# Branch phase in written order, and attention merges moved from the triangular inverse to the scan

## The chip, the cores and the metric

The kernel runs on one core of a Trainium2 chip. A core has TensorE (matrix products into the accumulators of PSUM), VectorE (DVE), ScalarE (ACT), GpSimd (POOL), and SyncE (SP), which here issues nearly all transfers between the device's main memory and the core's own memory SBUF. Each engine, and SP's queue of transfers, works through its instructions strictly in order: an instruction that waits holds up all that stand behind it on the same engine. The metric is the device time of one execution in microseconds (us); less is better.

## The reference, cut to what matters

One decoder layer over 2048 tokens of width 1024. Branch A is a gated delta rule with a 64-token chunk, which needs the inverse of a triangular 64 x 64 matrix per chunk and head, and then a scan over 16 pairs of chunks. Branch B is windowed attention in three groups with different dilation; the groups are merged by their softmax denominators. Both are gated, projected, merged by sigmoid gates, and projected out:

```
o_dn  = gated_delta_rule_chunked(dq, dk, dv, g, beta)        # inverse, then scan
y_dn  = (rms_norm(o_dn, dn_norm_w) * silu(dn_z)) @ w_branch_dn
outs, lses = three groups of dilated_window_attention(...)
alpha = softmax(stack(lses), axis=0)                          # the merge of groups
o_swa = sum(alpha[..., None] * stack(outs), axis=0)
y_swa = (o_swa * silu(swa_z)) @ w_branch_swa
merged = sigmoid(g_dn) * y_dn + sigmoid(g_swa) * y_swa        # the branch phase
x     = x + merged @ w_out                                    # the output groups
```

All of it is in float32. A product of two float32 matrices is made of three passes over operands split in a high and a low part (names ending in h and l).

## The kernel before

The program is written as a sequence of matmul loops with a clock of **ticks**. `hook()` advances the tick and runs whatever was booked with `at(delay, fn)` for that tick, so work for the other engines is written between the matmuls. `flush()` turns the clock without matmuls until nothing is booked. A planner then orders the instructions of each engine and of the transfer queue: it plays the program with its own costs and lets an instruction go when its inputs are ready, earlier-written ones first. Inside a `manual_schedule` block the named engines keep the written order instead; `pinned(False)` names TensorE, ACT, DVE and POOL, and `pinned(True)` SP's transfers as well.

The last stages, in order:

- **Units** (`cunits`, the matmuls of L723 to L725): 36 column blocks of the input projection, four pieces of 512 tokens each, 16 ticks a block. Beside the later ones run the inverse and the scan. A gate unit ends in `g_block` (L1158, a tanh on ACT) and a store to `gscr`; a weight block is split by ACT and POOL (L90, L91).
- **Inverse** (`inverse`, L1023 to L1026): 63 rows of ever longer DVE work. Row i books row i+1 after about its expected duration in ticks. The inverse starts 9 ticks into unit 15 (counted from 0). ACT and POOL keep the written order in it (the block `ipin`).
- **Merges** (`comb_setup`, `comb_load`, `comb_min`, `combine`): 16 merges, one for each 128 tokens. A merge loads 780 KB of group outputs (L1243, two buffers), takes the minimum on DVE (L1248), computes weights on POOL and ACT (L1259 to L1267), scales twelve tiles on ACT (L1271), adds them in two POOL operations (L1275) and stores the result to `osd`. Merge 0 starts 11 ticks after the setup, the others 15 ticks apart. The setup is called where the inverse starts.
- **Scan** (`scan`, L1061 to L1123): 16 steps of three ticks, the first 29 ticks after its start. A step's chain goes from TensorE to DVE (`rr`, L1087), TensorE (L1094), ACT (`vn`, L1096), TensorE (L1100) and DVE (`S`, L1102); a norm on ACT and POOL (L1112 to L1119) ends in a DVE scaling (L1121) and a store (L1123). `zs` (L1064) prepares the next step.
- **Branch phase** (`fin_y`): 8 blocks of 256 tokens, in each 8 tiles of 128 channels. A tile is two ticks: 12 matmuls for each branch (L1341 to L1343). Its gates come in a tile `gt` of 256 KB from `gscr` (`g_load`, L1329, seven buffers, issued four tiles ahead). DVE gates the product (L1345), POOL adds the branches (L1347), and SP stores 128 KB to `mscr` (L1348) out of the same `gt` buffer. For the next block `o_plan` loads `z` (L1303, three buffers) and `o` (L1293), transposes on TensorE at ticks 4, 7, 10 and 13 of the block (L1310), multiplies on DVE (L1311) and splits on ACT and POOL (L1314, L1315) into the operands of the block. In the first blocks `wo_chunk` prepares four chunks of the output weight, 28 ticks apart; the parts T1 and T4 go through the single buffers `th` and `tl` to main memory.
- **Output groups** (`group`, L1420): 8 groups of 84 matmuls.

The branch phase and the output groups are ordered by the planner alone. The pools of `th`, `tl` and of the second weight buffers open after those of the merges close.

Of the kernel before, what the change touches and what calls it, by code (L numbers as in the profile page):

```python
# [12 lines left out]
P = 128  # L13
# [34 lines left out]
class Net:  # L48
# [951 lines left out]
    def inverse(self, ip, done):  # L1000
# [12 lines left out]
        def row(i):  # L1013
            if i == 64:
                nc.sync.dma_start(dr(self.vscr, 0, [[4096, P], [1, 4096]]), M.rearrange("p c i -> p (c i)"))
                zt = Z.rearrange("p (i c) -> p i c", c=64)
                for r in (slice(0, 32), slice(32, 64)):
                    V.tensor_copy(zt[:, r, :], M.rearrange("p c i -> p i c")[:, r, :])
                nc.sync.dma_start(dr(self.tscr, 0, [[4096, P], [1, 4096]]), Z)
                done()  # L1020
                return
            pr = Z[:, :i * i].rearrange("p (c j) -> p c j", j=i)
            V.tensor_tensor(out=pr, in0=M[:, 0:i, 0:i], in1=M[:, i, 0:i].unsqueeze(1).to_broadcast([P, i, i]), op=ALU.mult)  # L1023
            V.memset(M[:, i, :], 0.0)
            V.memset(M[:, i, i:i + 1], 1.0)
            V.tensor_reduce(out=M[:, 0:i, i:i + 1], in_=pr, axis=mybir.AxisListType.X, op=ALU.add)  # L1026
            self.at(max(1, round((2 * i * i / 960.0 + 0.5) / 1.3)), lambda: row(i + 1))
# [205 lines left out]
    def comb_setup(self, cb):  # L1233
        self.cb = cb
        self.mone = cb.tile([P, 4], F32, name="mone", bufs=1)
        self.nc.gpsimd.memset(self.mone, -1.0)
        self.comb_load(0)
        self.at(6, self.comb_min)
        self.at(11, lambda: self.combine(0))

    def comb_load(self, t):
        oc = self.oc = self.cb.tile([P, G, H, 130], F32, name="oc", bufs=2)
        self.nc.sync.dma_start(oc.rearrange("p g h c -> p (g h c)"),  # L1243
                               dr(self.oscr, t * P * G * H * 130, [[G * H * 130, P], [1, G * H * 130]]))

    def comb_min(self):
        self.cs = self.cb.tile([P, 4, 12], F32, name="cs", bufs=2)
        self.nc.vector.tensor_reduce(out=self.cs[:, 0, 0:4].unsqueeze(2), in_=self.oc[:, :, :, 128].rearrange("p g h -> p h g"),  # L1248
                                     axis=mybir.AxisListType.X, op=ALU.min)

    def combine(self, t):
        nc, cb, V = self.nc, self.cb, self.nc.gpsimd
        oc, sm = self.oc, self.cs
        if t < 15:
# [28 lines left out]
        if t < 15:  # L1283
            self.at(9, self.comb_min)
# [46 lines left out]
    def fin_y(self, nb, m):  # L1331
        nc = self.nc
        self.g_load(8 * nb + m + 4)
# [14 lines left out]
        nc.sync.dma_start(dr(self.mscr, nb * P * 2048 + m * 256, [[2048, P], [1, 256]]), gt[:, 0, :])  # L1348
# [95 lines left out]
    def run(self):  # L1444
# [60 lines left out]
        pin, ipin = ExitStack(), ExitStack()  # L1505
# [10 lines left out]
        def start_inverse():  # L1516
            self.nb_out()
            pin.close()
            ipin.enter_context(tc.manual_schedule(engines={E.Activation, E.Pool}))
            dst.close()  # L1520
            self.comb_setup(pool(bst, "cb"))
            self.inverse(pool(ist, "ip", "right"), start_scan)

        def start_scan():
            ipin.close()
# [38 lines left out]
        for j in range(4):  # L1564
            self.g_load(j)
        for nb in range(8):
            if nb < 7:
                self.o_plan(nb + 1, 4)
            if nb == 0:
                for c in range(4):  # L1570
                    self.at(1 + 28 * c, lambda c=c: self.wo_chunk(c))
            if nb == 7:
                self.m_load(0)
            for m in range(8):
                self.fin_y(nb, m)
                if nb == 7 and m in (1, 3):
                    self.fetch("T1" if m == 1 else "T4")
                if nb == 7 and m < 4:
                    self.at(4, lambda m=m: self.m_op(m))
        self.flush()  # L1580
# [49 lines left out]
```

## Time and profile before

| | |
|---|---|
| time, median of 3 runs | 2402.06 us (2399.08 to 2407.04) |
| the profiled execution's own time | 2403.63 us |
| its span, from first to last instruction | 2401.8 us |
| granted TensorE clock, mean | 0.983 of full speed |
| TensorE busy | 2289.9 us, 95% of the span |
| DVE, ACT, POOL busy | 57%, 41%, 44% |
| transfers | 485.82 MB, mean 202 GB/s |
| first inverse work to last (DVE, L1023 to L1026) | to 1669.6 us |
| scan's matmuls (L1083) | 1702.5 to 1868.7 us |
| branch phase's matmuls | 1990.3 to 2238.1 us |

A row of a profile names the source line (L1341), the engine, and the tiles as output<-input. PE is TensorE, SPq the transfer queue of SP. A wait's row names who waited, on whom, us in total, times, and the longest. The granted clock is the share of full speed at which TensorE was allowed to run.

### The profile page before, as it was taken

Reading aid. Unit: us, or ns where it says so; the run is one execution under the profiler, and the core shown is the slowest. Engines: PE = TensorE matmul, PEld = TensorE weight load, DVE = VectorE, ACT = ScalarE, POOL = GpSimd, SP = SyncE. Lnnn points to the kernel's source line nnn. Section 1 sums busy time; section 2 is a strip of 40 time slices with the busy share of each in tenths; the row PEclk is TensorE's granted clock in tenths of the full one; section 3 lists DMA queues with packets and bytes.
Section 4 is the critical chain, followed back from the end, with each engine's and each line's share of the span. In section 5 each row is a group of like instructions: output and inputs, shape, how many; then the busy total and the mean of one; then the engine's idle time right before and its main releaser. Section 6 shows DMA issues by size and latency. Waiting matters only on the chain. (4 is left out here: it accounts for less than half of the span.)

```text
span 2401.8 us, 43873 instructions
## 1 busy us (share of the span) xinstructions
PE 2289.9 (95%) x15120; PEld 2078.5 (87%) x15120; DVE 1358.6 (57%) x2786; ACT 978.8 (41%) x3151; POOL 1050.3 (44%) x1460
## 2 busy tenths in 40 slices
PE   7999999989999999999999999998999998897999
PEld 7999999989999999787788788886888888896787
DVE  6566586693545545537777759997244114522553
ACT  5345466642434435445666633333443222200221
POOL 5374275574303213305567544666333214532543
PEclk8999999999999999999999999999999999998999
DMA  9989988858887888744545434444777637765742
GB/s 290 328 280 307 282 276 273 260 166 271 257 255 238 260 260 282 217 141 120 131 114 132 112 110 132 133 127 138 228 212 195 200 113 203 215 171 161 255 155 92
DMA packets 557270, 485.82 MB, mean 202 GB/s; under 512 B 68280, under 2 KB 517112, under 8 KB 554104
## 3 DMA queue, kind: packets, MB, share of 16 engines
q1 hardware_dynamic: 556760, 482.95, 66.0%
q8 instruction: 120, 1.97, 0.3%
q14 instruction: 102, 0.84, 0.1%
q10 hardware_dynamic: 288, 0.07, 0.0%
HBM read 280.23 MB, written 202.67 MB: 201 GB/s over the span
## 5 line engine op out<-in xcount | busy, mean ns | idle before, releaser
L723 PE MATMUL mm<-hh,w 128*128 128x512 f32 x1152 | 463.5, 402 | 7.6 <-ACT gt L1158 7.6
L725 PE MATMUL mm<-hh,w 128*128 128x512 f32 x1152 | 458.0, 398 | 1.6 <-POOL w L91 1.6
L724 PE MATMUL mm<-hl,w 128*128 128x512 f32 x1152 | 457.2, 397 | 0.0
L436 PE MATMUL mm<-w,hh 128*128 128x256 f32 x1760 | 327.9, 286 | 0.0
L436 PEld LDWEIGHTS mm<-w,hh 128*128 128x128 f32 x1760 | 270.9, 189 | 0.0
L723 PEld LDWEIGHTS mm<-hh,w 128*128 128x128 f32 x1152 | 220.4, 191 | 54.0 <-ACT gt L1158 8.0
L725 PEld LDWEIGHTS mm<-hh,w 128*128 128x128 f32 x1152 | 217.1, 188 | 49.1 <-POOL w L91 2.1
L436 PE MATMUL mm<-hh 128*128 128x256 f32 x880 | 256.4, 291 | 0.0
L724 PEld LDWEIGHTS mm<-hl,w 128*128 128x128 f32 x1152 | 217.5, 189 | 42.4
L436 PE MATMUL mm<-hl,hh 128*128 128x256 f32 x880 | 248.8, 283 | 0.4 <-POOL hl L298 0.3
L436 PE MATMUL mm<-hh,hl 128*128 128x256 f32 x880 | 248.6, 283 | 0.0
L436 PE MATMUL mm<-w,hl 128*128 128x256 f32 x880 | 248.1, 282 | 0.0
L91 POOL TENSOR_TENSOR w<-raw,w 128x512 fp32r<-128x512 f32 x68 | 103.3, 1522 | 224.0 <-ACT w L90 216.3
L610 DVE CUSTOM_DVE_ANT_0 p<-sc,mask 128x128 f32<-128x128 f32 (+1 forms) x192 | 70.1, 365 | 213.0 <-PE sc L607 83.4
L371 POOL TENSOR_SCALAR st<-st 128x4 f32<-128x4 f32 x96 | 20.9, 218 | 373.1 <-ACT junk L370 371.1
L436 PEld LDWEIGHTS mm<-hl,hh 128*128 128x128 f32 x880 | 168.2, 191 | 0.8 <-POOL hl L298 0.8
L436 PEld LDWEIGHTS mm<-hh 128*128 128x128 f32 x880 | 168.2, 191 | 0.0
L436 PEld LDWEIGHTS mm<-hh,hl 128*128 128x128 f32 x880 | 168.0, 191 | 0.0
L436 PEld LDWEIGHTS mm<-w,hl 128*128 128x128 f32 x880 | 165.9, 189 | 0.0
L594 ACT ACTIVATE kq<-tp 128x256 fp32r<-128x256 f32 x148 | 56.5, 381 | 183.1 <-PE tp L587 182.3
L837 DVE SCALAR_TENSOR_TENSOR acc<-xr,cw,acc 128x512 f32<-128x512 f32 x144 | 120.9, 840 | 17.3 <-ACT acc L835 11.8
L613 ACT ACTIVATE p<-p,ol 128x128 f32<-128x128 f32 (+1 forms) x192 | 88.1, 459 | 62.5 <-DVE ol L610 62.2
(352 smaller groups left out, 5888.9 us busy)
## 6 DMA issues: line engine op xcount, KB each, us to landing
wdr<-w SPq DMA_DIRECT2D x56, 512.0 KB, 4.9
w<-wdr SPq DMA_DIRECT2D x54, 512.0 KB, 5.3
qk<-qks SPq DMA_DIRECT2D x212, 128.0 KB, 4.0
qks<-rec SPq DMA_DIRECT2D x96, 256.0 KB, 3.0
raw<-in_w_in_dram SPq DMA_DIRECT2D x68, 256.0 KB, 3.7
gscr<-gt SPq DMA_DIRECT2D x64, 256.0 KB, 3.2
gt<-gscr SPq DMA_DIRECT2D x64, 256.0 KB, 4.1
wdr<-hh SPq DMA_DIRECT2D x28, 512.0 KB, 4.4
```

Source lines behind the costliest of these rows:

```text
L91: eng.tensor_tensor(out=l, in0=raw, in1=h.bitcast(F32), op=ALU.subtract)
L371: nc.gpsimd.tensor_scalar(out=st[:, 0:4], in0=st[:, 0:4], scalar1=1.0 / P, scalar2=EPS, op0=ALU.mult, op1=ALU.add)
L436: mm = lambda x, y, **kw: nc.tensor.matmul(o, x, y, skip_group_check=True, **kw)
L594: nc.scalar.activation(h, src, AF.Copy)
L610: nc.vector.tensor_tensor_reduce(out=p[:, lo:hi], in0=sc[:, lo:hi], in1=self.mask[:, slot * P + lo:slot * P + hi], scalar=3e38, scale=-SCA ...
L613: self.at(1, lambda: nc.scalar.activation(p[:, lo:hi], p[:, lo:hi], AF.Exp, bias=ol[:, 128:129], scale=-1.0, accum_out=ol[:, 129:130]))
L723: nc.tensor.matmul(pr, wh[:, k, :], a, start=(k == 0), stop=False)
L724: nc.tensor.matmul(pr, wh[:, k, :], b, start=False, stop=False)
L725: nc.tensor.matmul(pr, wl[:, k, :], a, start=False, stop=(k == KT - 1))
L837: nc.vector.scalar_tensor_tensor(out=acc, in0=xr[:, j:j + 512], scalar=w[:, j:j + 1], in1=acc, op0=ALU.mult, op1=ALU.add)
```

## The change

Two things are altered.

1. The branch phase's eight blocks and the flush after them run inside `pinned(True)`: all four engines and SP's transfers keep the written order. The store of a tile (L1348) is booked two ticks after the tile instead of being issued at once, and the gates are loaded three tiles ahead instead of four (three loads before the loop instead of four).
2. `comb_setup` is called at the end of the inverse (row 64), after its two stores are written and before the scan is; both first loads are issued there. A copy of one column of the inverse's result into each of the first two buffers makes their loads wait for the inverse. From merge 1 on, merge t issues the load of merge t+1 as before. The block `ipin`, in which ACT and POOL kept the written order during the inverse, is gone.

```
@@ inverse, row 64
                 nc.sync.dma_start(dr(self.tscr, 0, [[4096, P], [1, 4096]]), Z)
+                self.comb_setup(M)
                 done()
@@
-    def comb_setup(self, cb):
-        self.cb = cb
-        self.mone = cb.tile([P, 4], F32, name="mone", bufs=1)
+    def comb_setup(self, M):
+        self.M, self.ocs = M, {}
+        self.mone = self.cb.tile([P, 4], F32, name="mone", bufs=1)
         self.nc.gpsimd.memset(self.mone, -1.0)
         self.comb_load(0)
-        self.at(6, self.comb_min)
+        self.comb_load(1)
+        self.at(6, lambda: self.comb_min(0))
         self.at(11, lambda: self.combine(0))

     def comb_load(self, t):
-        oc = self.oc = self.cb.tile([P, G, H, 130], F32, name="oc", bufs=2)
+        oc = self.ocs[t] = self.cb.tile([P, G, H, 130], F32, name="oc", bufs=2)
+        if t < 2:
+            self.nc.vector.tensor_copy(oc[:, 0, 0, 0:1], self.M[:, 63, 63:64])
         self.nc.sync.dma_start(oc.rearrange("p g h c -> p (g h c)"),
...
     def combine(self, t):
         nc, cb, V = self.nc, self.cb, self.nc.gpsimd
-        oc, sm = self.oc, self.cs
-        if t < 15:
+        oc, sm = self.ocs.pop(t), self.cs
+        if 0 < t < 15:
             self.comb_load(t + 1)
...
         if t < 15:
-            self.at(9, self.comb_min)
+            self.at(9, lambda: self.comb_min(t + 1))
             self.at(15, lambda: self.combine(t + 1))
@@
     def fin_y(self, nb, m):
         nc = self.nc
-        self.g_load(8 * nb + m + 4)
+        self.g_load(8 * nb + m + 3)
...
-        nc.sync.dma_start(dr(self.mscr, nb * P * 2048 + m * 256, [[2048, P], [1, 256]]), gt[:, 0, :])
+        self.at(2, lambda: nc.sync.dma_start(dr(self.mscr, nb * P * 2048 + m * 256, [[2048, P], [1, 256]]), gt[:, 0, :]))
@@ run
-        pin, ipin = ExitStack(), ExitStack()
+        pin = ExitStack()
...
             pin.close()
-            ipin.enter_context(tc.manual_schedule(engines={E.Activation, E.Pool}))
             dst.close()
-            self.comb_setup(pool(bst, "cb"))
+            self.cb = pool(bst, "cb")
             self.inverse(pool(ist, "ip", "right"), start_scan)

         def start_scan():
-            ipin.close()
             ist.close()
...
-        for j in range(4):
+        for j in range(3):
             self.g_load(j)
-        for nb in range(8):
+        with pinned(True):
+            for nb in range(8):
...
-        self.flush()
+            self.flush()
         fst.close()
```

More of the change, by code (lines that the diff above doesn't have):

```diff
@@ L1231, in fetch, with comb_min @@
             self.nc.sync.dma_start(a.bitcast(F32).rearrange("p k c -> p (k c)"), dr(self.wpk[n, x], 0, [[2048, P], [1, 2048]]))
-    def comb_setup(self, cb):
-        self.cb = cb
-        self.mone = cb.tile([P, 4], F32, name="mone", bufs=1)
+    def comb_setup(self, M):
+        self.M, self.ocs = M, {}
+        self.mone = self.cb.tile([P, 4], F32, name="mone", bufs=1)
         self.nc.gpsimd.memset(self.mone, -1.0)
         self.comb_load(0)
-        self.at(6, self.comb_min)
+        self.comb_load(1)
+        self.at(6, lambda: self.comb_min(0))
         self.at(11, lambda: self.combine(0))
     def comb_load(self, t):
-        oc = self.oc = self.cb.tile([P, G, H, 130], F32, name="oc", bufs=2)
+        oc = self.ocs[t] = self.cb.tile([P, G, H, 130], F32, name="oc", bufs=2)
+        if t < 2:
+            self.nc.vector.tensor_copy(oc[:, 0, 0, 0:1], self.M[:, 63, 63:64])
         self.nc.sync.dma_start(oc.rearrange("p g h c -> p (g h c)"),
                                dr(self.oscr, t * P * G * H * 130, [[G * H * 130, P], [1, G * H * 130]]))
-    def comb_min(self):
+    def comb_min(self, t):
         self.cs = self.cb.tile([P, 4, 12], F32, name="cs", bufs=2)
-        self.nc.vector.tensor_reduce(out=self.cs[:, 0, 0:4].unsqueeze(2), in_=self.oc[:, :, :, 128].rearrange("p g h -> p h g"),
+        self.nc.vector.tensor_reduce(out=self.cs[:, 0, 0:4].unsqueeze(2), in_=self.ocs[t][:, :, :, 128].rearrange("p g h -> p h g"),
                                      axis=mybir.AxisListType.X, op=ALU.min)
@@ L1563, in run @@
         self.gt, self.mt, self.ss = {}, {}, {}
-        for j in range(4):
+        for j in range(3):
             self.g_load(j)
-        for nb in range(8):
[L1567 to L1579, printed above, removed]
-        self.flush()
+        with pinned(True):
+            for nb in range(8):
+                if nb < 7:
+                    self.o_plan(nb + 1, 4)
+                if nb == 0:
+                    for c in range(4):
+                        self.at(1 + 28 * c, lambda c=c: self.wo_chunk(c))
+                if nb == 7:
+                    self.m_load(0)
+                for m in range(8):
+                    self.fin_y(nb, m)
+                    if nb == 7 and m in (1, 3):
+                        self.fetch("T1" if m == 1 else "T4")
+                    if nb == 7 and m < 4:
+                        self.at(4, lambda m=m: self.m_op(m))
+            self.flush()
         fst.close()
```

## The prediction

> **What bounds the kernel now.** I read the page first, then stretches by stage, then waits and the order of time inside the two stretches where TensorE falls short.
>
> ```profile
> span 2401.8 us, 43873 instructions
> PE 2289.9 (95%) x15120; PEld 2078.5 (87%) x15120; DVE 1358.6 (57%) x2786; ACT 978.8 (41%) x3151; POOL 1050.3 (44%) x1460
> ```
>
> TensorE is the bound over the whole: no other engine passes 57%. A change can only win where TensorE waits or runs slowly. The table by stretches has, after the bounds and length, busy us (and count) of PE, PEld, DVE, ACT and POOL, then granted clock, DMA share and GB/s. The rows are the inverse, its end, the scan's start, the scan, the gate units after it, and the branch phase.
>
> ```profile
> 1425.00:1640.00 215.00, 215.00 (x932) 175.90 (x931) 203.60 (x270) 68.27 (x186) 119.99 (x99) 1.00 0.39 120
> 1640.00:1675.00 35.00, 25.77 (x105) 20.43 (x104) 22.82 (x16) 14.88 (x46) 25.29 (x27) 0.89 0.40 130
> 1675.00:1700.00 25.00, 25.00 (x109) 20.15 (x109) 3.44 (x3) 7.04 (x19) 11.21 (x17) 0.95 1.00 333
> 1697.50:1872.00 174.50, 166.80 (x1169) 145.35 (x1170) 70.85 (x232) 71.09 (x278) 58.93 (x172) 1.00 0.71 204
> 1872.00:1990.00 118.00, 118.00 (x528) 96.91 (x527) 19.11 (x32) 31.88 (x60) 23.30 (x25) 1.00 0.50 154
> 1990.30:2238.20 247.90, 210.05 (x1650) 206.93 (x1649) 93.89 (x126) 37.00 (x61) 109.04 (x107) 0.92 0.67 194
> ```
>
> The branch phase stands out: 37.9 us without a matmul and clock 0.92. Its own first matmuls show what it could be (order of time on PE), and two pieces of the chain of waits show the slow state after a stall.
>
> ```profile
> 1990.30 0.28 PE L1341 MATMUL mm<-oh,hh 128*128 128x256 f32 x1
> ...
> 1995.84 0.28 PE L1343 MATMUL mm<-oh,hl 128*128 128x256 f32 x1
> ```
>
> ```profile
> 2067.51 0.58 PE mm L1341
> 2068.09 0.21 PE mm L1342
> ...
> 2076.46 0.44 PE tp L1310 x4
> ```
>
> From 1990.30 to 1995.84 lie 47 steps: 0.118 us a matmul. After the stall that ends at 2067.51 a matmul takes 0.21. The phase has 8 blocks x 8 tiles x 24 = 1536 matmuls and 7 x 4 = 28 groups of four transposes: 1536 x 0.118 + 28 x 0.44 = 193.6 us. It takes 247.9, so **54.3 us are lost**, 37.9 as waits and 16.4 as slow clock.
>
> Who is waited for, by PE and then by the DMA queue, in 1990 to 2240 (us in total, times, longest), and the queue in order of time:
>
> ```profile
> PE mm L1341 <- DVE gt L1345: 15.8, 5, 8.4
> PE mm L1341 <- ACT w L1314: 7.9, 2, 4.3
> PE mm L1341 <- ACT th L90: 5.3, 1, 5.3
> PE mm L1342 <- POOL w L1315: 4.1, 3, 2.2
> PE mm L1341 <- ACT oh L1314: 2.7, 1, 2.7
> ```
>
> ```profile
> SPq L1329 <- DMA mscr<-gt: 98.2, 39, 4.5
> ```
>
> ```profile
> 2103.25 0.36 SPq L1329 DMA_DIRECT2D gt<-gscr  x1
> 2103.70 0.42 SPq L1348 DMA_DIRECT2D mscr<-gt  x1
> ...
> 2107.46 0.36 SPq L1329 DMA_DIRECT2D gt<-gscr  x1
> ```
>
> 39 of 64 gate loads stand at the head of the queue until a store of a gate tile has landed: the load at 2107.46 goes out 3.76 us after the store just before it. One load per tile then takes about 4.2 us, where TensorE needs 24 x 0.118 + 0.5 x 0.44 = 3.05. Everything behind a waiting load (z, o) is late too, which is why the second group of waits names the operands (L1314, L1315), not the gates.
>
> **The change, part by part.**
>
> *Stores two ticks later, loads one tile less ahead, all in source order.* A tick here is half a tile, 12 x 0.118 = 1.42 us, and a tile with its share of transposes 3.05. In source order the queue sees load(i+3), store(i-1), load(i+4), store(i). With seven buffers load(i+4) needs the landing of store(i-3), issued two tiles, 6.1 us, before store(i-1). Landings, from the page:
>
> ```profile
> gt<-gscr SPq DMA_DIRECT2D x64, 256.0 KB, 4.1
> ```
>
> A store of half the size should not need longer than 4.1, so load(i+4) finds its buffer free, and as store(i-1) goes about 2 us after its tile's end (gating on DVE, sum on POOL), the load has five tiles less 2 us, 13 us, until DVE wants it. Pinning adds waits: each store waits in place for POOL's sum, and the fourth z load of a block (three buffers, tick 5) for POOL's subtraction of the first (tick 4). Behind them stand gate loads with that lead and o loads with more: nothing; without it, the old 1.2 us a tile. The first z load of a block goes at tick 1 for tick 4, 4.3 us: it comes some 2 us late, DVE stands, gatings behind it, and three accumulators (two tiles, 6 us) cover that. What is late next is the operand chain: the last transposes of a block come at tick 13 and their result is used at tick 17, 4 x 1.42 = 5.7 us on, for a chain of
>
> ```profile
> L1311 DVE SCALAR_TENSOR_TENSOR z<-tp,z 128x512 f32<-128x512 f32 x14 | 9.6, 687 | 23.9 <-DMA z<-zscr 20.0 <-PE tp L1310 2.4 <-PE mm L1343 1.6
> L1314 ACT ACTIVATE w<-z 128x512 fp32r<-128x512 f32 x16 | 10.0, 630 | 64.9 <-DVE z L1311 64.9
> L1315 POOL TENSOR_TENSOR w<-z,w 128x512 fp32r<-128x512 f32 x16 | 21.3, 1333 | 21.1 <-ACT w L1314 18.1 <-DVE gt L1345 2.9
> ```
>
> 0.44 + 0.69 + 0.63 + 1.33 = 3.1 us, with one or two gate operations of 0.7 ahead of it, and the weight chunks' subtractions in four of the blocks. So some of the 20.0 us of operand waits (7.9 + 5.3 + 4.1 + 2.7) stay. Bounds for what is left of 54.3: none, or 20.0 x 54.3 / 37.9 = 28.7 with its share of slow clock. I take 14, the middle: the z loads' lateness went with the gate loads, the tight 5.7 us did not. **Branch: -40.3** (-54 to -26). DMA has room: 0.67 x 247.9 = 166 us of full work in 193.6 + 14 = 208 is a share of 0.80.
>
> The Trainium skill ("TensorE: Matmul & The Clock Gate", Part 1) says that the clock falls back only after an idle window of about 3.4 us. By it remaining waits of 1 to 3 us would cost no slow clock and the residue would be nearer 10 than 14; the trace bears it out that the 5 us stall above was followed by 0.21.
>
> *Merges out of the inverse.* At its end DVE, ACT and PE stand in a row behind one late merge load (1640 to 1676 for DVE and ACT, 1640 to 1700 for PE):
>
> ```profile
> DVE cs L1248 <- DMA oc<-oscr: 12.0, 3, 7.3
> ```
>
> ```profile
> ACT cs L1262 <- POOL cs L1259: 21.8, 2, 11.1
> ```
>
> ```profile
> PE mm L723 <- ACT gt L1158: 7.6, 1, 7.6
> ```
>
> A matmul of the units takes 215 / 932 = 0.231 us; 105 of them are 24.2 of the 35 us, so 10.8 are lost. With no merge there, and ACT and POOL free to reorder, DVE's rows and the evictions remain, which lost nothing before 1640. Bounds -10.8 to 0; I take **-10**.
>
> *Merges beside the scan.* Two merges lay there already, and DVE's and POOL's order of time shows their price:
>
> ```profile
> 1707.37 0.43 DVE L1064 TENSOR_TENSOR zs<-sc,nbr 64x256 f32<-64x256 f32 x1 [2.28 <-PE sc L1061]
> ...
> 1717.40 1.47 DVE L1121 TENSOR_SCALAR os<-qs,oss 128x128 f32<-128x128 f32 x2 [1.04 <-POOL oss L1119]
> ...
> 1721.09 0.43 DVE L1064 TENSOR_TENSOR zs<-sc,nbr 64x256 f32<-64x256 f32 x1 [1.19 <-PE sc L1061]
> ...
> 1728.01 0.48 DVE L1121 TENSOR_SCALAR os<-qs,oss 128x128 f32<-128x128 f32 x2 [1.04 <-POOL oss L1119]
> ...
> 1731.39 0.43 DVE L1064 TENSOR_TENSOR zs<-sc,nbr 64x256 f32<-64x256 f32 x1 [1.85 <-PE sc L1061]
> ```
>
> ```profile
> 1717.32 1.27 POOL L1275 TENSOR_TENSOR oc<-oc 128x512 f32<-128x512 f32 x1
> ```
>
> ```profile
> 1795.22 0.43 DVE L1064 TENSOR_TENSOR zs<-sc,nbr 64x256 f32<-64x256 f32 x1 [1.80 <-PE sc L1061]
> 1807.69 0.43 DVE L1064 TENSOR_TENSOR zs<-sc,nbr 64x256 f32<-64x256 f32 x1 [1.19 <-PE sc L1061]
> ```
>
> L1064 opens a scan step. A plain step is 10.3 us (1721.09 to 1731.39); the two with a merge are 13.7 and 12.5, mean +2.8. While POOL adds (L1275) a DVE normalisation pair takes 1.47, not 0.48, and the scan's next product stands behind it on DVE. How many merges land in the scan now? By ticks the scan takes 29 + 48 = 77 after the inverse and merge k starts at 11 + 15k, so five start in it (k = 0 to 4). The queue's rows of before speak for ticks rather than for a merge as soon as a buffer is free: the last two loads are 81 us apart.
>
> ```profile
> 1704.53 0.44 SPq L1243 DMA_DIRECT2D oc<-oscr  x1
> 1785.60 0.60 SPq L1243 DMA_DIRECT2D oc<-oscr  x1
> ```
>
> Ends: two as now, or all but the first two, 14. I take five: 3 x 2.8 = **+8.4** (0 to +33.6). The other eleven fall into the 118 us after the scan, where DVE was busy 19 and ACT 32: nothing, if they fit; the rival below is that they do not. The two loads of 780 KB ahead of the scan's loads are 1.6 MB / 333 GB/s = 4.8 us of a full DMA: 0 to 5, I take **+1**, as TensorE has units to run and the planner puts the scan where it expects the data. The two copies of one column lie in DVE's idle time before the scan's first step.
>
> The Trainium skill ("SBUF — State Buffer", Who interferes with whom) calls this an exclusive lock: a DVE operation in a two-port mode and a GpSimd operation block each other for the whole instruction. It speaks against this move: by it every add that meets L1121 costs up to 1.27, 2.5 a merge, and the trace's 1.47 agrees.
>
> *Sum.* -40.3 - 10 + 8.4 + 1 = -40.9. The profiled execution took 2403.63 us (1.83 of it outside the span of 2401.8), so 2362.7; the median of the runs is 2402.06, 1.57 lower: **2361**.
>
> **The rivals.**
>
> *Crowd in the scan.* The planner starts merges as soon as a buffer is free, and 14 lie in the scan: 33.6 instead of 8.4, 2361 + 25.2 = 2386. For it: the compute of the merge at 1710 ran well before its tick. Against: the 81 us to the next load.
>
> *Operands late.* Source order leaves the operand waits as they are: residue 28.7 instead of 14, 2376. For it: 5.7 us against 3.1 and a DVE queue that must also do the weight chunks; against: 20.0 of the 23.9 us that DVE stood before L1311 were for late z loads.
>
> *Landings set the pace.* The branch phase is limited by DMA, not by order: no gain there, 2401. Against: share 0.67, and a single landing of about 4 us is what each load waits for.
>
> *Merges outlast the units (slower).* The inverse begins 9 ticks into the 16th of 36 units of 16 ticks, so 21 x 16 - 9 = 327 ticks of units remain; its rows' delays take 169, and 158 are left for the merges, which start at 11 + 15k: ten start, six are left to the drain. If each is then done alone, it takes from its load (1704.53 above) to the end of its last add
>
> ```profile
> 1721.66 1.29 POOL L1275 TENSOR_TENSOR oc<-oc 128x512 f32<-128x512 f32 x1 [3.07 <-ACT oc L1271]
> ```
>
> 18.4 us: 110 us into the branch phase. The tiles th and tl of the weight chunks come into the room of the merge's pool, ACT copies into th at tick 12 and in source order all later operand copies stand behind it; TensorE is out of operands after the first block, at 24.4 us, and waits 86: 2361 + 86 = 2447. It makes the change slower from the point where merges last more than 24.4 + 41 = 65 us past the units. Against: ACT, DVE and the queue are nearly idle for 118 us, in which pairs of merges need 11 x 9.2 = 101.
>
> **How the numbers follow.** Forecast 0.64 (own range 2344 to 2375: residue 5 to 22, scan 0 to +14), crowd 0.13, operands late 0.12, landings 0.04, outlasting 0.07. For the range I leave out the slower rival and part of the ends: 2343 to 2388. A change under 0.3% can't be told from none; landings fall there, outlasting is slower, the rest is faster: 0.89, 0.04, 0.07.
>
> **What would show it.** Right: in the branch phase no waits of L1329 for mscr<-gt, clock near 1.00, length near 207 us; no PE wait for L1158 before the scan; scan steps of 12 to 14 us in about five places. Wrong: PE waits on ACT th or L1314 at block starts; merges (L1248) after the first L1341; scan steps of 13 us throughout; a branch phase above 225.

## The result, and the profile after

The changed kernel takes 2376.09 us (median of 4 runs, 2375.21 to 2379.8), the kernel before beside it 2402.06 (median of 3). One further run of the kernel before (2768.38 us) and one of the ten of e12 below (3702.22) fell into a slow state and are not counted. The ratio is 0.989, with a 95% interval of 0.987 to 0.992: 26 us are gained, where 41 were forecast. The profiled execution took 2375.45 us, 28.2 less than that of before.

The page's first lines, and the table by stretches (bounds, length, busy us and count of PE, PEld, DVE, ACT and POOL, granted clock, DMA share, GB/s), of the changed kernel; the rows are the inverse, its end, the scan's start, the scan, the units after it, and the branch phase:

```profile
span 2373.6 us, 43873 instructions
...
PE 2282.9 (96%) x15120; PEld 2069.9 (87%) x15120; DVE 1353.3 (57%) x2788; ACT 979.7 (41%) x3151; POOL 1004.8 (42%) x1460
```

```profile
1425.00:1643.00 218.00, 218.00 (x944) 178.40 (x944) 210.65 (x268) 34.91 (x59) 35.34 (x20) 1.00 0.23 72
1643.00:1673.00 30.00, 30.00 (x131) 24.30 (x130) 8.69 (x9) 7.01 (x19) 9.82 (x19) 1.00 0.94 314
1673.00:1700.00 27.00, 22.24 (x133) 19.38 (x134) 5.74 (x19) 11.95 (x41) 9.57 (x24) 0.87 0.48 147
1697.50:1872.00 174.50, 165.48 (x1128) 143.46 (x1127) 69.39 (x224) 76.38 (x294) 67.00 (x184) 0.99 0.71 204
1872.00:2002.70 130.70, 115.72 (x481) 91.86 (x480) 14.71 (x29) 63.27 (x175) 66.46 (x96) 0.96 0.67 208
2002.70:2207.30 204.60, 197.29 (x1649) 196.31 (x1648) 97.38 (x130) 37.98 (x64) 110.09 (x107) 0.98 0.81 242
```

The inverse's end has no gap and a clock of 1.00. The branch phase is 204.6 us long instead of 247.8. But the stretch before it, where TensorE had been busy without a break (118.00 of 118.00), now has 15.0 us without a matmul and a clock of 0.96. Its waits say why, in the view of waits of PE over the whole span (us in total, times, longest):

```profile
PE mm L723 <- ACT gt L1159: 13.7, 7, 4.1
...
PE mm L1345 <- DVE gt L1349: 7.1, 4, 4.3
```

All seven waits of the first row lie between 1855 and 2003 us: TensorE's unit matmuls (L723) wait until ACT has emptied an accumulator (the gate eviction, L1159, which was L1158 before).

The stretches of a window hold different amounts of work, so the difference is read from the same work in both kernels. TensorE starts 1152 matmuls at L723, counted from 0. Number 800 lies in the inverse, and from there on I count the time to number 900 (the inverse's end), 1000 (scan), 1100 and 1151 (units after the scan), then the branch phase (first matmul of it to the first of the output groups) and the groups to the end of the span, all in us from the start times in the trace:

| kernel | to 900 | to 1000 | to 1100 | to 1151 | branch | groups | span |
|---|---|---|---|---|---|---|---|
| before | 92.5 | 167.1 | 71.1 | 35.4 | 247.8 | 163.7 | 2401.8 |
| after | 85.5 | 171.1 | 86.3 | 41.9 | 204.6 | 166.3 | 2373.6 |
| difference | -7.0 | +4.0 | +15.2 | +6.5 | -43.2 | +2.6 | -28.2 |

The remaining 6.2 us lie before number 800, and 5.6 of them are there at the first matmul of L723 (972.2 us instead of 977.8), long before anything that was changed. Number 800 came at 1615 to 1624 us in the profiled executions of all the kernels below, so a single profile has about 4 us of scatter on either side from there.

How ACT comes to hold up TensorE is to be seen in the order of time of ACT and of PE in the changed kernel (start, us, engine and line, operation, tiles, count, idle time before and its releaser):

```profile
1911.56 0.21 ACT L1266 ACTIVATE cs<-cs 128x12 f32<-128x12 f32 x1 [3.99 <-POOL cs L1263]
1914.05 1.28 ACT L1275 ACTIVATE oc<-oc,cs 128x128 f32<-128x128 f32 x4 [2.28 <-POOL cs L1271]
1915.23 0.58 ACT L1159 ACTIVATE gt<-mm 128x512 f32<-128x512 f32 x1
```

```profile
1904.70 0.40 PE L725 MATMUL mm<-hh,w 128*128 128x512 f32 x1
1905.93 0.50 PE L723 MATMUL mm<-hh,w 128*128 128x512 f32 x1 [0.83 <-ACT gt L1159]
...
1915.86 0.79 PE L723 MATMUL mm<-hh,w 128*128 128x512 f32 x1 [4.10 <-ACT gt L1159]
1916.45 0.63 PE L724 MATMUL mm<-hl,w 128*128 128x512 f32 x1
```

There are three accumulators. The piece that starts at 1915.86 takes that of the piece three before it, which was complete before 1904.70. From 1907.6 on ACT did nothing for 3.99 us and again for 2.28 us, but an exponential and four scalings of a merge stood ahead of the eviction, and they waited for POOL's weights (L1263, L1271). POOL in turn had waited for a minimum on DVE (L1252), which stood 15.04 us, until 1911.06, for its merge's load. An engine that is idle holds up the bound, because it is idle at the head of a queue. After the stall the next matmul comes 0.59 us later, where 0.23 is the pace.

The eleven late merges do lie where they were forecast (the last addition is at 1975 us, ahead of the branch phase), and five lie in the scan; the sixth begins beside its last step (exponential at 1861.4). What they cost there is that TensorE goes at the pace of ACT's order.

### The profile page after: what moved, and what is told of

Same layout as the page of the kernel before. It is cut to its first block, busy times and chain, and to the rows that moved or that the text cites. A ratio compares the mean times of both kernels' runs of the same rounds, so it can differ in the third digit from the quotient of the medians.

```text
span 2373.6 us, 43873 instructions
## 1 busy us (share of the span) xinstructions
PE 2282.9 (96%) x15120; PEld 2069.9 (87%) x15120; DVE 1353.3 (57%) x2788; ACT 979.7 (41%) x3151; POOL 1004.8 (42%) x1460
## 5 line engine op out<-in xcount | busy, mean ns | idle before, releaser
L723 PE MATMUL mm<-hh,w 128*128 128x512 f32 x1152 | 464.8, 403 | 13.7 <-ACT gt L1159 13.7
L723 PEld LDWEIGHTS mm<-hh,w 128*128 128x128 f32 x1152 | 220.7, 192 | 62.0 <-ACT gt L1159 16.7
L91 POOL TENSOR_TENSOR w<-raw,w 128x512 fp32r<-128x512 f32 x68 | 99.2, 1461 | 361.8 <-ACT w L90 361.6
L370 ACT ACTIVATE junk<-rec 128x128 f32<-128x128 f32 x288 | 89.4, 310 | 54.9 <-DVE rec L364 47.3
```

The lines of the kernel that those rows point to most:

```text
L91: eng.tensor_tensor(out=l, in0=raw, in1=h.bitcast(F32), op=ALU.subtract)
L370: nc.scalar.activation(self.junk, src[:, j * P:(j + 1) * P], AF.Square, accum_out=st[:, j:j + 1])
L723: nc.tensor.matmul(pr, wh[:, k, :], a, start=(k == 0), stop=False)
```

## The experiments

An edit of the kernel before keeps its line numbers, one of the changed kernel those of after; where an edit adds lines, those behind it move (L1278 and L1274 of e4 are L1275 and L1271 of after, L1346 and L1350 of e7 are L1345 and L1349). The ratio is always to the kernel before, measured beside it on the same chip.

**e1: the branch phase alone.** The kernel before with part 1 of the change (pinned, store two ticks later, loads three ahead), the merges left where they were.

```
-        self.g_load(8 * nb + m + 4)
+        self.g_load(8 * nb + m + 3)
...
-        nc.sync.dma_start(dr(self.mscr, ...), gt[:, 0, :])
+        self.at(2, lambda: nc.sync.dma_start(dr(self.mscr, ...), gt[:, 0, :]))
...
+        with pinned(True):
+            for nb in range(8):
...
```

> Only the first part: branch phase in written order, store two ticks later, loads three ahead; the merges stay beside the inverse. Theory (the two parts add up; the branch phase is worth -42.7, the move of the merges costs about +15 after its own gain at the inverse): 2404 - 43 = 2361, ratio 0.982, and the 10.8 us lost at the inverse's end are still lost. Rival (the branch phase gains only because the merges moved, or the merges' move is itself a gain of 10): 2375 to 2385.

Measured: 2360.96 us, ratio 0.983 (0.981 to 0.985). Branch 205.0, to 1100 and 1151 71.1 and 35.4 as before. The gain of part 1 alone is 42 us. Its waits of PE from 1640 to 2010 us still have that of before at the inverse's end, as the merges stand where they stood:

```profile
PE mm L723 <- ACT gt L1158: 7.2, 1, 7.2
```

**e2: the merges alone.** The kernel before with part 2.

```
                 nc.sync.dma_start(dr(self.tscr, 0, ...), Z)
+                self.comb_setup(M)
...
-            ipin.enter_context(tc.manual_schedule(engines={E.Activation, E.Pool}))
-            self.comb_setup(pool(bst, "cb"))
+            self.cb = pool(bst, "cb")
```

> Only the second part: merges beside the scan; the branch phase as the planner orders it. Theory: -7 at the inverse, +20 to +25 from the scan's start to the end of the units (gate evictions on ACT stand behind merges), branch phase still 245 to 250: 2404 + 16 = 2420, ratio 1.007. Rival (the merges' move is a gain of 10 as forecast with the inverse, and the loss after the scan belongs to the pinned branch phase, for which the planner holds engines back): 2394.

Measured: 2424.44 us, ratio 1.010 (1.007 to 1.012): the move of the merges is a loss of 22 us by itself. Inverse's end 85.6, scan 173.4, units after it 88.2 and 41.2, branch 248.6. The two parts give -42 + 22 = -20 us together; the change's ratio with its interval is -32 to -20 us, so that the sum lies at its edge: the parts add up within the noise.

**e3: scaling of the late merges on DVE.** The changed kernel; from merge 5 on, the twelve scalings (L1275) run on DVE.

```
+                if t < 5:
                     nc.scalar.activation(oc[...], oc[...], AF.Identity, scale=c[...])
+                else:
+                    nc.vector.tensor_scalar(out=oc[...], in0=oc[...], scalar1=c[...], scalar2=None, op0=ALU.mult)
```

> The changed kernel with the scaling of merges 5 to 15 on DVE (12 x 128x128 tensor_scalar) instead of ACT; only the exponential of a merge (0.2 us) is left on ACT. Theory (evictions wait on ACT behind the scaling, which waits for POOL's weights and the merge's load): of the 20 us lost from the scan to the end of the units 10 to 20 come back: 2356 to 2366. Rival (the whole row of waits hangs on the late load, and the exponential alone holds ACT as long): 2374 to 2380.

Measured: 2376.38 us, ratio 0.990 (0.988 to 0.993), the same as the change. The units after the scan take 7.6 us less (81.9 and 38.7), the scan 6.2 more (177.3); from number 900 to 1151 it is 297.9 instead of 299.3. So the busy time of the scaling was at most a part of what held ACT. Its wait for POOL grew instead, at the one instruction that was left there (waits of ACT from 1875 to 2000 us):

```profile
ACT cs L1266 <- POOL cs L1263: 65.3, 9, 9.0
```

In the changed kernel itself the same view has

```profile
ACT cs L1266 <- POOL cs L1263: 25.9, 9, 5.2
ACT oc L1275 <- POOL cs L1271: 20.4, 9, 3.2
```

so ACT's waits of 46 us in total became one of 65: an in-order engine is blocked by what it waits for as well as by what it does.

**e4: no loads for the late merges.** The changed kernel; from merge 5 on the 780 KB are not loaded but filled with ones on DVE. So eleven of the 16 merges work on ones instead of the groups' outputs: that part of the computation is left out.

```
+        if t >= 5:
+            self.nc.vector.memset(oc, 1.0)
+            return
         self.nc.sync.dma_start(oc.rearrange("p g h c -> p (g h c)"), ...
```

> The changed kernel with the loads of merges 5 to 15 left out (DVE fills the buffer with ones instead, so those merges compute on ones). Theory (after the scan, evictions on ACT stand behind a merge's exponential, which waits by way of POOL and DVE for the merge's load, later than the planner assumed): the waits of the exponential for POOL, 25.9 us in 1875 to 2000, and PE's 13.7 us for L1159 nearly go, and the stretch from the scan to the end of the units shortens by 15 to 20 of its 21.6 us: 2356 to 2361. Rival (the chain of POOL and ACT inside a merge holds ACT long enough without any load): 2370 or more.

Measured: 2375.39 us, ratio 0.990 (0.989 to 0.992). Units after the scan 88.3 and 35.4; from number 900 to 1151 298.8 instead of 299.3. TensorE still waits 7.3 us for L1159 (13.7 in the change), and the time is the same: the late load is not what it hangs on. With no load to wait for, the merges follow one another directly (exponentials at 1912.58, 1920.47 and 1928.36, 7.9 us apart), and ACT waits inside each for POOL's second set of weights (waits of ACT, 1860 to 2000 us):

```profile
ACT oc L1278 <- POOL cs L1274: 32.4, 10, 5.9
```

**e7: ACT and POOL in written order from the scan's end.** The changed kernel; from the end of the scan to the branch phase ACT and POOL keep the written order, and the merges that are left come 9 ticks apart.

```
+            self.at(8 if late else 9, lambda: self.comb_min(t + 1))
+            self.at(9 if late else 15, lambda: self.combine(t + 1))
...
+            upin.enter_context(tc.manual_schedule(engines={E.Activation, E.Pool}))
+            self.late = True
...
+        upin.close()
```

> The changed kernel with ACT and POOL in written order from the end of the scan to the branch phase, and the merges written there 9 ticks apart (minimum 8 ticks after the load), so that they end with the units. Theory (the planner put merge steps ahead of evictions on ACT on a guess of the load's landing; in written order a merge's steps come when the load has had 8 ticks, 11 us): PE's wait for L1159 goes, 2356 to 2361. Rival (merges beside the units cost TensorE whatever the order, by ACT's and POOL's time): 2372 to 2380.

Measured: 2382.19 us, ratio 0.993 (0.991 to 0.994). The units after the scan take 71.1 and 35.4, as before: the whole 21.7 us come back when an eviction stands where it was written, and no wait for L1159 is left. But merge 5 came only at tick 86 after the inverse, and 86 + 10 x 9 = 176 ticks are more than the 158 that there are: additions (L1279 here) run until 2026 us, the branch phase begins at 1984.7, and DVE's gating comes late. The additions from 1980 us on (operation, count, durations in ns, first and last start) and the waits of PE in 1980 to 2230 us:

```profile
L1279 POOL TENSOR_TENSOR oc<-oc x8: 1265/1283/1744, 1981.7 to 2025.8; 128x512 f32<-128x512 f32 x8
```

```profile
PE mm L1346 <- DVE gt L1350: 26.6, 5, 12.1
```

The branch phase takes 227.2 instead of 204.6. This is the prediction's "merges outlast the units", and it costs 23 us for an overhang of 41.

**e11: the same order, all merges 9 ticks apart.** As e7, with the 9 ticks from the first merge on.

```
-            self.at(9, lambda: self.comb_min(t + 1))
-            self.at(15, lambda: self.combine(t + 1))
+            self.at(8, lambda: self.comb_min(t + 1))
+            self.at(9, lambda: self.combine(t + 1))
...
+            upin.enter_context(tc.manual_schedule(engines={E.Activation, E.Pool}))
...
+        upin.close()
```

> The changed kernel with ACT and POOL in written order from the end of the scan on, and all merges written 9 ticks apart, so that the last ends 4 ticks before the units (in the run with late spacing the units lost nothing, but merges ran 41 us into the branch phase). Theory (after the scan the changed kernel loses 21.6 us because the planner's order on ACT ties evictions to the chain of merges, at 8 us a merge; spaced out in written order they cost nothing): no PE wait for L1159, branch phase 205, two or three more merges in the scan at 1 to 3 us each: 2354 to 2364. Rival (merges beside the units cost TensorE wherever they lie): 2372 or more.

Measured: 2371.76 us (2363.69 to 2372.57), ratio 0.986 (0.984 to 0.988); the profiled execution is the fastest of them, with a span of 2361.8. Seven merges lie in the scan (175.6), the units take 74.4 and 35.4, the branch phase 203.4, and the last addition, at 1985.5, is before it. By stages 18 of the 21.7 us are mended, and with two more merges in the scan 4.5 of them are lost again: 14 better than the change. The medians are 4 us apart and the ratios 8, so the theory's 2354 to 2364 is met by the profiled execution alone; where the rest went stays open. Order and spacing change together in e7 and e11, since merges written 15 ticks apart would not end with the units; the written order by itself was not tried.

**e6: the queue to the planner.** The changed kernel with `pinned(False)`: the four engines keep the written order, SP's transfers do not.

```
-        with pinned(True):
+        with pinned(False):
```

> The changed kernel with the four engines in written order in the branch phase, but SP's transfers ordered by the planner. Theory (the queue's order is what cured the gate loads): gate loads stand again behind landings of stores, and 20 to 40 of the 42.7 us are lost again: 2396 to 2418. Rival (the engines' order, the delayed store and the shorter lead are enough): 2376 or less.

Measured: 2402.37 us, ratio 1.001 (0.999 to 1.002). The time is in the range that the theory gave, but not for its reason. The gate loads stand at the queue's head as before (SP's waits, 2015 to 2230 us):

```profile
SPq L1333 <- DMA mscr<-gt: 84.7, 39, 4.9
```

and still the branch phase is only 211.7 us long, 7 more than after. Another 8 are lost at the start of the output groups (174.6), where TensorE waits for one step of ACT (waits of PE from 2227 us on):

```profile
PE mm L1424 <- ACT hold L1403: 7.2, 1, 7.2
```

The rest of the 26 us lies in the scan and in the units (177.5, 90.8), which the edit does not touch by itself; why the planner orders them otherwise was not traced.

**e8: store at once, all in source order.** The changed kernel with the store (L1352) issued with its tile and the loads four tiles ahead.

```
-        self.g_load(8 * nb + m + 3)
+        self.g_load(8 * nb + m + 4)
...
-        self.at(2, lambda: nc.sync.dma_start(dr(self.mscr, ...), gt[:, 0, :]))
+        nc.sync.dma_start(dr(self.mscr, ...), gt[:, 0, :])
```

> The changed kernel with all four engines and the queue in written order, but the store of a tile issued at once and the gates loaded four tiles ahead, as before. Branch phase of the changed kernel 204.6 us, of the kernel before 247.8. Theory (written order of engines and queue does it; a store in place holds the queue only until POOL's sum): 204 to 212. Rival (the store's two ticks are needed: the queue stands at each store until POOL has ended, and z and o loads come late): 220 to 235.

Measured: 2394.26 us, ratio 0.995 (0.994 to 0.997). The branch phase takes 219.0, 14 more than after: the theory of this run failed, and its rival, though 1 us short of its range, is seen in the rows below. The gates' lateness is gone here too; what is late is z. SP's waits in the branch phase of e8, and DVE's:

```profile
SPq L1352 <- POOL gt L1351: 80.5, 33, 8.0
```

```profile
DVE z L1315 <- DMA z<-zscr: 40.7, 6, 12.0
...
DVE gt L1349 <- DMA gt<-gscr: 2.1, 1, 2.1
```

In the changed kernel stores wait 40.0 us for POOL's sum, half of that, and z is late by 26.3.

**e9: no order at all.** The changed kernel without the pinned block; store two ticks later and loads three ahead remain.

```
-        with pinned(True):
-            for nb in range(8):
+        for nb in range(8):
...
```

> The changed kernel with its delayed store and its lead of three tiles, but the branch phase ordered by the planner altogether. Theory (the written order of the four engines gave most of the branch phase's gain, since with SP's order planned alone its length was still 211.7): branch phase 235 to 250, time 2405 to 2425. Rival (the delayed store and the shorter lead give it, whatever the order): branch phase 205 to 215, time 2376 to 2400.

Measured: 2427.5 us, ratio 1.010 (1.007 to 1.012), as e2. Branch 249.0. Store and lead by themselves do nothing for it.

**e12: the engines' order alone.** Store at once, loads four ahead, and `pinned(False)`.

```
-        self.g_load(8 * nb + m + 3)
+        self.g_load(8 * nb + m + 4)
...
-        with pinned(True):
+        with pinned(False):
```

> The changed kernel with the four engines in written order, the queue ordered by the planner, the store at once and the lead of four tiles as before. Theory (the engines' order is the cure, and the stores' two ticks matter little): branch phase 208 to 218. Rival (order of engines and delayed store are both needed): 230 to 248.

Measured: 2396.2 us, ratio 0.997 (0.996 to 0.998). Branch 212.2, groups 173.9. The six kernels with the moved merges that differ from the branch phase on, then, with the sum of branch phase and groups in brackets:

| | store at once, 4 ahead | store 2 ticks later, 3 ahead |
|---|---|---|
| planner alone | e2: 2424.44 (413.1) | e9: 2427.5 (415.8) |
| engines in written order | e12: 2396.2 (386.1) | e6: 2402.37 (386.3) |
| engines and queue | e8: 2394.26 (385.8) | after: 2376.09 (370.9) |

The engines' order is worth 27 to 30 us of it, with either store. The queue's order is worth 15 more, and only together with the later store and the shorter lead, which were always changed together. What the engines' order takes away is to be seen in DVE's waits in the branch phase. Before:

```profile
DVE gt L1345 <- PE mm L1343: 47.0, 21, 6.4
DVE gt L1345 <- DMA gt<-gscr: 30.7, 9, 4.0
DVE z L1311 <- DMA z<-zscr: 20.0, 6, 5.6
DVE raw L1206 <- DMA raw<-in_w_out_dram: 16.8, 4, 12.1
```

and in e12, with the same store, the same lead and again 39 waits of gate loads for stores (87.4 us):

```profile
DVE z L1315 <- DMA z<-zscr: 27.3, 6, 8.0
...
DVE gt L1349 <- DMA gt<-gscr: 14.3, 6, 3.4
```

The fourth row of before is absent in e12, as it is in e6. It is a weight chunk's subtraction (`wo_chunk`), and the order of time on DVE of the kernel before shows what stood behind it, and its chain of waits where the load came from:

```profile
2066.16 0.69 DVE L1206 TENSOR_TENSOR raw<-raw,raw 128x512 f32<-128x512 f32 x1 [12.11 <-DMA raw<-in_w_out_dram]
2066.77 0.68 DVE L1345 SCALAR_TENSOR_TENSOR gt<-gt,mm 128x512 f32<-128x512 f32 x1
```

```profile
2060.83 0.37 SPq L1329
2061.25 4.82 DMA raw<-in_w_out_dram
```

The planner had put the subtraction ahead of a gating, and a wait of TensorE of 4.81 us ends at 2067.51, when this gating is done. The subtraction's load had left right behind a gate load, so in this stall the order on DVE and the order of the queue meet. The longest wait of the phase, 8.4 us, ends at 2219.12 in the same way: the gating stood behind a sum for the first output groups (L1376), which had waited 9.99 us for its load from `mscr`.

**b1: merges beside the inverse alone, 10 ticks apart.** e1, with a third buffer for a merge's input, loads two merges ahead, and merges 10 instead of 15 ticks apart. The setup stays where the kernel before has it, and so does the block `ipin`; the merges' pool is closed at the scan's end.

```
-        oc = self.oc = self.cb.tile([P, G, H, 130], F32, name="oc", bufs=2)
+        oc = self.ocs[t] = self.cb.tile([P, G, H, 130], F32, name="oc", bufs=3)
...
-            self.comb_load(t + 1)
+            self.comb_load(t + 2)
...
-            self.at(9, self.comb_min)
-            self.at(15, lambda: self.combine(t + 1))
+            self.at(7, lambda: self.comb_min(t + 1))
+            self.at(10, lambda: self.combine(t + 1))
```

> The branch phase of the change, with the merges left beside the inverse (ACT and POOL in written order there, as before), but with three buffers, each load written two merges ahead, and merges 10 ticks apart, so that all 16 are written within the inverse; the merges' pool closes where the scan ends. Theory (the inverse's end lost its 10.8 us to one late load, and two merges in the scan cost 5.6): 2361 - 10.8 - 5.6 = 2345. Rival (merges beside the inverse stall evictions again at another place, or hold DVE's rows up so that the scan comes late): 2361 or more.

Measured: **2344.39 us, ratio 0.977** (0.975 to 0.979), the best of all. The merges run from 1443 to 1655 us, none in the scan: inverse's end 84.4, scan 160.2, units 71.1 and 35.4, branch 202.4. The stretch of the inverse, where all of them now lie, and its end:

```profile
1425.00:1640.00 215.00, 215.00 (x932) 175.87 (x932) 202.50 (x276) 89.22 (x254) 145.92 (x140) 1.00 0.47 146
1640.00:1670.00 30.00, 30.00 (x131) 24.57 (x130) 29.62 (x14) 9.32 (x23) 19.56 (x12) 1.00 0.46 150
```

TensorE does not miss a step in either. POOL and ACT had room there: 145.92 and 89.22 of 215 us, in the written order.

**b2: the same, 15 ticks apart.** Only the two delays of b1 stay at 9 and 15.

```
-        oc = self.oc = self.cb.tile([P, G, H, 130], F32, name="oc", bufs=2)
+        oc = self.ocs[t] = self.cb.tile([P, G, H, 130], F32, name="oc", bufs=3)
...
-            self.comb_load(t + 1)
+            self.comb_load(t + 2)
```

> As the one before, with the merges 15 ticks apart as in the kernel before: only the third buffer and the earlier load differ from the branch phase alone. Theory (late load): the wait of TensorE for L1158 near 1664 goes, merges at the scan stay: 2361 - 10.8 = 2350. Rival (not the load, but DVE's minimum standing behind the long rows): 2361.

Measured: 2363.03 us, ratio 0.985 (0.983 to 0.987), as e1. The third buffer and the earlier load alone do not help, and one load is late even so (DVE waits 8.6 us for it); the merges reach to 1695 us, and TensorE waits at the inverse's end (waits of PE, 1640 to 2010 us), which takes 101.9:

```profile
PE mm L723 <- ACT gt L1158: 14.1, 3, 6.8
```

b1 and b2 differ in the spacing alone. What b1 gains by, then, is that the merges are over before the inverse ends (its last row on DVE is at 1665 us in b1, at 1681 in b2).

## Why the prediction was right, and where it failed

**The forecast of 2361 was 15 us too low**; the time lies in its range of 2343 to 2388. That owes something to luck. The forecast's own range ended at 2375, and the room above it was there for rivals that did not come: 2376 is the very time of "operands late", but TensorE's waits for operands in the branch phase are 0.2 us in total. And the loss of 21.7 us where none was expected is offset in part by 5.4 on the scan's term and by 6.2 of scatter. By its terms, against the table of stages:

| term | forecast | measured |
|---|---|---|
| branch phase | -40.3 | -43.2 (e1: -42 in the median) |
| inverse's end | -10 | -7.0 |
| merges in the scan, and the first loads | +9.4 | +4.0 |
| the other eleven merges | 0 | +21.7 |
| output groups | 0 | +2.6 |
| before unit matmul number 800 | 0 | -6.2, scatter |

**The step that failed** is "The other eleven fall into the 118 us after the scan, where DVE was busy 19 and ACT 32: nothing, if they fit". They fit, and cost 21.7 us all the same. The prediction asked whether there was room, by busy time; it did not ask in which order the room would be used. Less than half of the stretch's 130.7 us are busy on ACT even now (63.27), but for another 46 ACT waits for POOL inside the merges, and the evictions stand behind. Taking away the load (e4) or the scaling (e3) changes the time by under 1 us; writing the order down (e7, e11) brings the units back to 106.5 and 109.8 from 128.2. The prediction itself had the view at hand that speaks against "nothing": TensorE's wait of 7.6 us for L1158 at the inverse's end, which it put down to a late load, was an eviction behind the scaling of one merge on ACT. The load was late there, but it was the order on ACT that passed the lateness on.

**The branch phase came out right in size, and half right in reason.** The waits of gate loads for stores are nearly gone in the changed kernel, 3.8 us instead of 98.2 (SP's waits, 1970 to 2220 us):

```profile
SPq L1352 <- POOL gt L1351: 43.3, 32, 6.1
...
SPq L1333 <- DMA mscr<-gt: 3.8, 5, 1.7
```

with a clock of 0.98 and a length near the 207 us foretold. But 39 of 64 loads at the head of the queue were not by themselves what cost the 54.3 us: e6 has the same 39 and a branch phase of 211.7. Most of it was the planner's order on the engines; of TensorE's waits in the phase, those for DVE fall from 15.8 us to 1.9 in e6, those for operands of ACT and POOL from 20.0 to 11.4. Which engine's order counts most was not tried by itself. The queue's order adds 7 in the phase and 8 after it. The part "the z loads' lateness went with the gate loads, the tight 5.7 us did not" came out the other way round. The operand waits went (0.2 us are left), and the z loads' lateness stayed (26.3 us of DVE's waits, 20.0 before):

```profile
DVE gt L1349 <- PE mm L1347: 37.3, 18, 9.4
DVE z L1315 <- DMA z<-zscr: 26.3, 5, 7.2
```

The first row says that DVE mostly waits for TensorE, as it did before (47.0). The second is what is left to cost time. The longest wait of the phase comes of it, in the order of time of DVE and then PE:

```profile
2166.75 0.75 DVE L1315 SCALAR_TENSOR_TENSOR z<-tp,dnw,z 128x512 f32<-128x512 f32 x1 [7.22 <-DMA z<-zscr]
...
2169.98 1.27 DVE L1349 SCALAR_TENSOR_TENSOR gt<-gt,mm 128x512 f32<-128x512 f32 x2
```

```profile
2170.80 0.36 PE L1345 MATMUL mm<-oh,hh 128*128 128x256 f32 x1 [4.27 <-DVE gt L1349]
```

The gatings stood behind a z that was 7.22 us late and two steps of a weight chunk after it, and that is more than the 6 us of three accumulators by which the prediction had a late z covered. The residue was taken as 14 and is 11.0: 7.3 us without a matmul and 3.7 of slow clock. The prediction weighed a rule of the Trainium skill here ("TensorE: Matmul & The Clock Gate", Part 1): after an idle window of about 3.4 us the clock falls back. By it, shorter waits would cost no slow clock. The rows at the end of this document show that a wait of 2.06 us can already bring it, so that counting slow clock into the residue was right in kind.

**Merges in the scan.** Five, as the ticks said. The stage grew by 4.0 us, where 9.4 were taken for the three more merges and the first loads. A price per merge can't be read from that: kernels whose scan is written as in the change take 171.1 to 177.5 for it (e2, e6 to e9, e12), e1 166.7 with two merges, b1 160.2 with none. Not all of the difference is the merges' own work, either. DVE's slowest pair of L1122 in the changed kernel's scan meets no addition of a merge but two weight splits (L91) of POOL:

```profile
1836.26 2.52 DVE L1122 TENSOR_SCALAR os<-qs,oss 128x128 f32<-128x128 f32 x2 [1.04 <-POOL oss L1120]
```

```profile
1836.18 2.52 POOL L91 TENSOR_TENSOR w<-raw,w 128x512 fp32r<-128x512 f32 x2
```

A pair that takes 0.48 alone takes 2.52 here, and the scan's step with it lasts 16.8 instead of 10.3. The steps are less even than "12 to 14 us in about five places": the longest is 20.0, at the scan's start. That TensorE lost only 4.0 us on the same count of unit matmuls fits with these filling a longer step; it was not tried by itself.

**The rivals.** Operands late, landings and the crowd in the scan did not come. The slower one came in a kernel of its own, e7, when the merges were written 9 ticks apart too late: its place was right (the head of the branch phase), though it shows in the gating on DVE rather than in the copies of ACT that it named. Its rule, the overhang less 24.4 us, gives 17 us for e7's overhang of 41; measured are 23.

## What to carry to other kernels

Room on a side engine is not measured by its busy time: on an engine that works in order, count for each side chain how long it stands at the head waiting for another engine, and ask which instruction of the bound engine's supply stands behind it. A long wait at the head of a queue is a symptom until a run removes it alone: here 39 such waits stayed, and two thirds of the gain came all the same. And side work did best here where the written order leaves room between the pieces (b1: all merges inside the inverse, at 10 ticks), not where the engines' totals are lowest.

## What was not expected of the hardware

Landings got slower while the phase got faster: the gate loads' median from issue to landing is 5.3 us in the changed kernel (4.1 before), with DMA busy 0.81 of the branch phase instead of 0.67 and 242 GB/s instead of 194:

```profile
gt<-gscr SPq DMA_DIRECT2D x64, 256.0 KB, 5.3
```

With a lead of three tiles DVE waits 1.7 us for it in the whole phase, instead of 30.7.

The slow clock goes by fixed windows, not by the length of a wait alone. PE's order of time in the changed kernel after two waits of the units, and stretches of 3.41 us with the granted clock (the third figure from the end) around these waits and around the wait of 4.27 us above:

```profile
1930.21 0.50 PE L723 MATMUL mm<-hh,w 128*128 128x512 f32 x1 [1.58 <-ACT gt L1159]
...
1938.10 0.50 PE L723 MATMUL mm<-hh,w 128*128 128x512 f32 x1 [2.06 <-ACT gt L1159]
```

```profile
1929.16:1932.57 3.41, 2.36 (x10) 1.97 (x11) 0.17 (x1) 1.76 (x6) 2.64 (x4) 1.00 0.35 118
1932.57:1935.99 3.42, 3.42 (x15) 2.48 (x14) 0.00 (x0) 1.66 (x6) 2.93 (x6) 1.00 0.26 77
1935.99:1939.40 3.41, 1.35 (x7) 1.09 (x7) 0.00 (x0) 3.23 (x10) 2.27 (x2) 1.00 0.75 227
1939.40:1942.82 3.42, 3.42 (x10) 2.65 (x9) 0.17 (x1) 0.21 (x1) 2.21 (x6) 0.50 0.76 260
...
2168.10:2171.51 3.41, 0.71 (x6) 0.74 (x7) 2.80 (x4) 1.10 (x3) 1.99 (x3) 1.00 0.31 88
2171.51:2174.93 3.42, 3.42 (x18) 3.42 (x18) 0.94 (x2) 0.63 (x1) 3.42 (x5) 0.50 0.67 195
```

The records of the granted clock in the 14 traces have only 1.00 and 0.50, and past the program's first microseconds each of their 167 slow stretches lasts 3.41 us or two to four times that. All of them begin and end on one grid of 3.41 us in each execution. The wait of 1.58 us is split by the grid (the window from 1929.16 has 2.36 us of work), and the next window is at full clock. The wait of 2.06 us lies within one window, which has 1.35 us of work, and the next is slow, though TensorE had restarted 1.3 us before. In all 14 executions between 1880 and 2200 us a window at full clock with up to 1.59 us of work was always followed by a slow one, and one with more than 1.65 never (1236 windows). That is a little less than half of a window. A slow window costs about 1.6 us, 8 unit matmuls of 0.43 us where 15 of 0.23 would go, and a wait of 4 us no more than that on top. The Trainium skill's 3.4 us, in the rule named above, is the length of the window here, and a window need be idle for little more than its half.

The wait of 7.2 us ahead of the output groups in e6 appears where the engines are in written order and the queue is the planner's, in e12 too (6.4 us). What leads to it was not tried by itself.
